# Sums of squares with the ones stationary, and roots that travel by way of HBM, in one layer of a hybrid decoder trunk

## The chip, the core and the metric

The kernel runs on one core of a Trainium2 chip. A core has a matrix engine (TensorE, PE in the profile, which reads its stationary operand by weight loads, PEld), a vector engine (VectorE, DVE), a scalar engine (ScalarE, ACT), a general engine (GpSimd, POOL) and a queue engine (SyncE, SP). Each takes its instructions in order. Transfers between HBM and the on-chip memory are issued from the queues of SP, ACT and POOL. The metric is the device time of one execution in microseconds, lower is better; the median of three runs before is 676.56 us.

## The reference

One decoder layer on 512 tokens of width 1024. After a modulated RMSNorm one projection feeds two token mixers. The second of them, differential attention, is where the change lies:

```python
scores = jnp.einsum('bqhmd,bshmd->bhmqs', qblk, k).astype(jnp.float32) * scale
...
p = jax.nn.softmax(scores, axis=-1)
a = p[:, :, 0] - lam * p[:, :, 1]
return jnp.einsum('bhqs,bshe->bqhe', a.astype(v.dtype), v)
...
out = _rmsnorm(out, subln_g) * (1.0 - lam_init)
```

There are four heads of 128 value columns. Each head's output is normalised for each token: its 128 values are squared and summed, the mean plus a small constant goes under a root, and the values are multiplied by the inverse root, a gain per column and a constant. Both mixers' outputs are then projected, gated and merged, projected again and added to the input; a gated MLP and a last RMSNorm follow.

## The kernel before

Everything is float32; large products are made of three passes over operands split into a high part that TensorE takes at full speed and a low part (`split`, `mm3`: high times high, high times low, low times high). The split of each weight tile is one cast on ScalarE and one subtraction on VectorE.

From line 513 the order of TensorE's instructions is written by hand. `fill(n)` advances a stream of background products (query and key projections, gates of the first mixer `pga`, its branch `pA`, gates of the second `pgd`, its branch `pB`) by n ticks, a tick being three passes of 512 columns; between the ticks the attention's own products are placed. `after(n, fn)` has `fn` issued n ticks later. The orders of VectorE, ScalarE and POOL in this stretch are chosen by a planner from priorities (`tc.high_priority`) and from bounds such as `tc.issue_after`, which keeps an instruction behind another on the same engine.

`diff_values(h)` (line 727) makes a head's output with the value columns on the partitions and the 512 tokens along the free dimension, in the one bank of the tag "v". ScalarE squares it into `sq` and copies it, with the gain, into `of`. STAT_LAG (6 ticks) later `stats` runs:

- Four matmuls (line 746), one for each block of 128 tokens, with the block of squares stationary and one column of ones moving: they leave the sums as a 128x4 block, tokens on partitions, in a "v" bank `pss`.
- `rstd_start` on VectorE (line 156) scales these and adds `e0`, the small constant times the squared softmax denominator, which POOL makes in lines 749 and 750; POOL takes the power of -1/2 (line 158) and four steps that refine it (lines 755 to 758), and writes four columns of the tile `cols`.
- ROW_LAG (8, 8, 6, 7) ticks after the statistic `to_rows` (line 100) turns columns of `cols` on TensorE, ScalarE copies the last 32 rows to `part`, and two DMAs issued from POOL write the four rows to HBM (2 KB) and read them back to all 128 partitions as `rb`, 128x512 (256 KB).
- NORM_LAG (34, 34, 34, 24) ticks after the statistic `spread` multiplies `of` by `rb` on VectorE (line 768) and splits the product into the head's places in `vvh` and `vvl`. For heads 0 to 2 the multiply is kept behind the next head's statistic step (`summed[h + 1]`).

The branch `pB` of the second mixer (`add_merge`, line 958) reads `vvh` and `vvl` of all four heads, head by head. `to_rows` serves the two gates of the residual adds too (`g1`, `g2`).

Of the kernel before, what the change touches and what calls it, by code (L numbers as in the profile page):

```python
# [8 lines left out]
F32 = mybir.dt.float32  # L9
F32R = mybir.dt.float32r  # L10
AF = mybir.ActivationFunctionType
ALU = mybir.AluOpType
PSUM = bass.MemoryType.PSUM

P = 128
# [3 lines left out]
NT = S // P  # L19
DFF = 2816  # L20
FT = DFF // P
EPS = 1e-6
# [5 lines left out]
HP = 100000  # L28
# [6 lines left out]
ROW_LAG = (8, 8, 6, 7)  # L35
# [4 lines left out]
NCOL = 161  # L40
G1COL = NCOL + 16
# [6 lines left out]
def kernel(  # L48
# [19 lines left out]
    nc = tc.nc  # L68
# [3 lines left out]
    def pool(name, bufs=1, space=None, stack=ctx):  # L72
        kw = {} if space is None else {"space": space}
        return stack.enter_context(tc.tile_pool(name=name, bufs=bufs, reuse_waits="tile", **kw))

    cpool = pool("const")
# [3 lines left out]
    dp = pool("rows", space=bass.MemoryType.DRAM)  # L80

    def bank(tag, bufs, shape, name, dt=F32):
        return ps.tile(shape, dt, tag=tag, bufs=bufs, name=name)
# [10 lines left out]
    def vbank(name, shape=(P, S)):  # L94
        return bank("v", 1, list(shape), name)
# [4 lines left out]
    def to_rows(dst, lo, n, name):  # L100
        turned = vbank(name, (P, P))
        nc.tensor.transpose(turned, cols[:, lo + n - P : lo + n], ident)
        part = cpool.tile([32, P], F32, tag="part", name=name + "p")
        with tc.high_priority(offset=2 * HP):
            nc.scalar.copy(part, turned[96:])
        d = dp.tile([n, P], F32, name=name + "d")
        nc.gpsimd.dma_start(d, part[32 - n :])
        nc.gpsimd.dma_start(dst, d.rearrange("k q -> (k q)").partition_broadcast(P))
# [10 lines left out]
    def split(hi, lo, src):  # L119
        return nc.scalar.copy(hi, src), nc.vector.tensor_sub(lo, src, hi.bitcast(F32))  # L120

    def mm3(o, lh, ll, rh, rl, start, stop):
        nc.tensor.matmul(o, lh, rh, start=start, stop=False)  # L123
        nc.tensor.matmul(o, lh, rl, start=False, stop=False)  # L124
        nc.tensor.matmul(o, ll, rh, start=False, stop=stop)  # L125
# [4 lines left out]
    ones = cpool.tile([P, P], F32, name="ones")  # L130
# [5 lines left out]
    mhalf = cpool.tile([P, 4], F32, name="mhalf")  # L136
# [3 lines left out]
    cols = cpool.tile([P, NCOL + 64], F32, name="cols")  # L140
# [8 lines left out]
    root_in = [None]  # L149

    def rstd_start(ssq, n, d, wpool, plus=None):
        ms = wpool.tile([P, n], F32, tag="rs_a", bufs=3, name="ms")
        if plus is None:
            nc.vector.tensor_scalar(ms, ssq, 1.0 / d, EPS, ALU.mult, ALU.add)
        else:
            root_in[0] = nc.vector.scalar_tensor_tensor(ms, ssq, 1.0 / d, plus, ALU.mult, ALU.add)
        r0 = wpool.tile([P, n], F32, tag="rs_c", bufs=3, name="r0")
        nc.gpsimd.tensor_tensor(r0, ms, mhalf[:, :n], ALU.pow)
        return ms, r0
# [74 lines left out]
    def keep_warm(n):  # L234
        for i in range(n):
            nc.tensor.matmul(acc[5][:, :P], ones, ones, start=True, stop=True)
# [12 lines left out]
    nc.gpsimd.affine_select(ddf, ddf, [[-1, 512]], ALU.is_ge, NEG, base=384, channel_multiplier=1)  # L249
    eps = cpool.tile([P, 1], F32, name="eps")  # L250
    nc.gpsimd.memset(eps, EPS)

    keep_warm(10)
    cs = cpool.tile([P, 8], F32, name="cs")
# [56 lines left out]
    for p in range(KT // 2):  # L311
        for hf in range(2) if p == 3 else (None,):
            sl = ALL if hf is None else HALVES[hf]
            sq, xx = (a.rearrange("p (a s) -> p a s", a=2)[:, :, sl] for a in (sqs[p], xT[:, p]))
# [15 lines left out]
    r0 = pp.tile([P, NT], F32, tag="rs_c", bufs=3, name="r0")  # L330
    nc.scalar.activation(r0, stat[:, :, 0], AF.Sqrt, bias=eps, scale=1.0 / D)
    ms = pp.tile([P, NT], F32, tag="rs_a", bufs=3, name="ms")
# [59 lines left out]
    for k in range(KT):  # L392
        n = k + 1
# [24 lines left out]
    ap = pool("att", stack=at)  # L418
# [129 lines left out]
    def after(n, fn):  # L548
        later.append([n, fn])
# [175 lines left out]
    emptied, summed = {}, {}  # L725

    def diff_values(h):
        aTh, aTl = aTs[h]
        o = vbank(f"od{h}")
        for k in range(NT):  # L730
            q0 = k * P
            mm3(
                o[:, q0:], vv[0][:, h, k * P : (k + 1) * P], vv[1][:, h, k * P : (k + 1) * P],
                aTh[:, k * AW + q0 : k * AW + 512], aTl[:, k * AW + q0 : k * AW + 512],
                k == 0, k == NT - 1,
            )
        sq = big.tile([P, S], F32, tag="sq2", name=f"sq{h}")
        of = big.tile([P, S], F32, tag=("kvA", "kvB")[h % 2], name=f"of{h}")
        with tc.high_priority(offset=HP):
            nc.scalar.activation(sq, o, AF.Square)  # L740
            emptied[h] = nc.scalar.activation(of, o, AF.Copy, scale=sublnc)

        def stats():
            pss = vbank(f"pss{h}", (P, NT))
            for n in range(NT):
                nc.tensor.matmul(pss[:, n : n + 1], sq[:, n * P : (n + 1) * P], ones[:, 0:1], start=True, stop=True)
            rs = cols[:, NCOL + NT * h : NCOL + NT * h + NT]
            l0, e0 = sums[h][:, 0], sums[h][:, 1]
            nc.gpsimd.tensor_tensor(e0, l0, l0, ALU.mult)
            nc.gpsimd.tensor_scalar_mul(e0, e0, EPS)  # L750
            with tc.high_priority(offset=HP):
                ms, r0 = rstd_start(pss, NT, P, ap, plus=e0)
                summed[h] = root_in[0]
                t = ap.tile([P, NT], F32, tag="rs_b", bufs=3, name="rt")
                nc.gpsimd.tensor_tensor(t, r0, r0, ALU.mult)
                nc.gpsimd.tensor_tensor(t, t, ms, ALU.mult)
                nc.gpsimd.tensor_scalar_add(t, t, -3.0)
                nc.gpsimd.tensor_tensor(rs, t, r0, ALU.mult)
            last = h == DIFF_HEADS - 1
            rb = big.tile([P, S], F32, tag="sq2", name="rb3") if last else ap.tile([P, S], F32, tag="rb", name=f"rb{h}")  # L760

            def spread():
                with ExitStack() as place:
                    for b in recent:
                        place.enter_context(tc.issue_after(b.ins))
                    if not last:
                        place.enter_context(tc.issue_after(summed[h + 1].ins))
                    nc.vector.tensor_mul(of, of, rb)
                with tc.high_priority(offset=HP), ExitStack() as place:
                    if not last:  # L770
                        place.enter_context(tc.issue_after(emptied[h + 1].ins))
                    split(vv[0][:, h], vv[1][:, h], of)

            after(ROW_LAG[h], lambda: to_rows(rb, NCOL + NT * h, NT, f"rs{h}"))
            after(NORM_LAG[h], spread)

        after(STAT_LAG[h], stats)


# [114 lines left out]
    for s in range(4 * DIFF_HEADS):  # L894
        h, n = divmod(s, NT)
# [368 lines left out]
    ssq, r2, xns = {}, {}, {}  # L1264
# [614 lines left out]
```

## Time and profile before

| | |
|---|---|
| median of three runs | 676.56 us (676.55 to 677.2) |
| profiled execution, first to last instruction | 675.4 us |
| mean granted clock of TensorE | 0.996 |
| sums of squares (line 746), four heads | start at 149.42, 174.56, 199.00, 216.90 us |
| multiply by the roots (line 768) | starts at 178.88, 202.85, 219.85, 235.29 us |
| first `pB` | starts at 238.52 us |

The page gives busy time for each engine, the view of windows the same for stretches of the span with the granted clock of TensorE and the DMA's share. Groups of instructions stand by line, output and inputs. A row of the timeline gives the start, the length, the engine and line, the operation and its shapes, how many were merged (x8), and in brackets how long the engine had been idle and who released it. Starts are the more telling on TensorE, where neighbours overlap. The list of DMA issues gives size and median time from issue to landing. The chain that ended last is merged in the same way. One float32 matmul of these statistics is issued as two passes, each with a weight load, so four stand as x8.

### The profile page before, as it was taken

To read this page: it belongs to the slowest core of one execution; us is meant where nothing else is said; L and a number is where in the kernel's file an instruction comes from. 1 tells how busy PE (TensorE), PEld (TensorE's weight loads), DVE (VectorE), ACT (ScalarE), POOL (GpSimd) and SP (SyncE) were. 2 spreads that over 40 slices of the span, in tenths; PEclk is the share of its full clock that TensorE was granted. 3 is DMA by queue.
4 is the path that set the end of the run, shared out by engine and by line. 5 is a ranking of instruction groups with operands and counts; after the bars stand their busy time and mean duration, and the time that the engine had idled before them with its cause. 6 is when DMAs were issued, how large, how long until landed. Compare 5 with 4: busy or idle time off the path is not lost.

```text
span 675.4 us, 10797 instructions
## 1 busy us (share of the span) xinstructions
PE 665.2 (98%) x4021; PEld 591.5 (88%) x4021; DVE 564.1 (84%) x1005; ACT 400.6 (59%) x704; POOL 85.0 (13%) x111
## 2 busy tenths in 40 slices
PE   8999999999999999999999999999999999999995
PEld 7888888888887888888899999999999998888884
DVE  6988997778767678954899998888888899979996
ACT  7678787465745333233696655556655666665664
POOL 2000000002213100010010211011111004441200
PEclk9999999999999999999999999999999999999998
DMA  9961231445255697568365988797886559996803
GB/s 357 417 235 62 94 95 63 132 149 179 89 170 188 236 314 264 189 185 282 92 123 137 227 201 200 203 214 162 187 198 171 132 187 208 198 203 186 157 0 125
DMA packets 72068, 121.78 MB, mean 180 GB/s; under 512 B 4240, under 2 KB 48432, under 8 KB 72016
## 3 DMA queue, kind: packets, MB, share of 16 engines
q1 hardware_dynamic: 53104, 95.04, 41.4%
q0 software_dynamic: 18624, 25.84, 22.8%
q8 instruction: 31, 0.51, 0.3%
q10 hardware_dynamic: 288, 0.21, 0.1%
q14 instruction: 21, 0.17, 0.1%
HBM read 118.97 MB, written 2.11 MB: 179 GB/s over the span
## 4 chain that ended last, share of the span: by engine, by line
PE 84%; issue 7%; DVE 4%; DMA 1%; ACT 1%; POOL 1%; POOLq 0%; ACTq 0%
PE up L1202 33%; PE dc L1808 7%; PE av L371 3%; PE oc L1262 2%; PE oc L1258 2%; PE pgd L124 2%; PE pgd L123 2%; PE oc L1259 2%; PE pgd L125 2%; PE aqa L368 2%; PE pga L123 1%; PE pga L125 1%; PE pga L124 1%; PE sw L581 1%; PE sd L679 1%
## 5 line engine op out<-in xcount | busy, mean ns | idle before, releaser
L1202 PE MATMUL up<-t,m_whi 128*128 128x256 f32 x512 | 93.1, 283 | 0.0
L1202 PEld LDWEIGHTS up<-t,m_whi 128*128 128x128 f32 x512 | 79.9, 192 | 0.0
L1202 PE MATMUL up<-t,m_wlo 128*128 128x256 f32 x256 | 72.4, 283 | 0.0
L1202 PE MATMUL up<-bh,p_whi 128*128 128x256 f32 x232 | 65.7, 283 | 0.0
L1202 PE MATMUL up<-bl,p_whi 128*128 128x256 f32 x232 | 65.7, 283 | 0.0
L1202 PE MATMUL up<-bh,p_wlo 128*128 128x256 f32 x232 | 65.7, 283 | 0.0
L1202 PEld LDWEIGHTS up<-t,m_wlo 128*128 128x128 f32 x256 | 49.2, 192 | 0.0
L1104 POOL DMA_DIRECT2D s<-in_w_up_dram x21 | 27.0, 1367 | 158.5 <-DMA s<-in_w_up_dram 104.8
L1202 PEld LDWEIGHTS up<-bh,p_whi 128*128 128x128 f32 x232 | 44.5, 192 | 0.0
L1202 PEld LDWEIGHTS up<-bl,p_whi 128*128 128x128 f32 x232 | 44.5, 192 | 0.0
L1202 PEld LDWEIGHTS up<-bh,p_wlo 128*128 128x128 f32 x232 | 44.5, 192 | 0.0
L1132 ACT CAST m_whi<-s 128x1024 fp32r<-128x1024 f32 x31 | 32.5, 1048 | 15.7 <-DVE s L1126 9.1
L795 DVE CUSTOM_DVE_ANT_0 ra<-ra,csb 128x1024 f32<-128x1024 f32 x32 | 38.6, 1219 | 3.8 <-DMA ra<-in_w_ada_t_dram 3.7
L1136 DVE TENSOR_TENSOR m_wlo<-s,m_whi 128x1024 fp32r<-128x1024 f32 x31 | 37.7, 1217 | 1.3 <-ACT m_whi L1132 1.3
L1202 PE MATMUL up<-t,p_whi 128*128 128x256 f32 x176 | 32.2, 283 | 0.0
L1202 PEld LDWEIGHTS up<-t,p_whi 128*128 128x128 f32 x176 | 27.4, 192 | 0.1
L705 ACT ACTIVATE sd<-sd,dmx 128x128 f32<-128x128 f32 (+3 forms) x32 | 17.8, 556 | 14.9 <-DVE dmx L690 14.7
L1132 ACT CAST p_whi<-wa 128x1024 fp32r<-128x1024 f32 x18 | 18.8, 1042 | 12.6 <-PE up L1202 9.0
L1209 ACT ACTIVATE gT<-a,cols 128x512 f32<-128x512 f32 x22 | 17.6, 813 | 13.4 <-DVE a L1244 13.0
L1136 DVE TENSOR_TENSOR p_wlo<-wa,p_whi 128x1024 fp32r<-128x1024 f32 x18 | 22.0, 1222 | 4.0 <-ACT p_whi L1132 2.7
L1202 PE MATMUL up<-t,p_wlo 128*128 128x256 f32 x88 | 24.9, 283 | 0.0
L1126 DVE TENSOR_TENSOR s<-s,wa 128x1024 f32<-128x1024 f32 x20 | 24.3, 1217 | 0.1
(551 smaller groups left out, 2036.4 us busy)
## 6 DMA issues: line engine op xcount, KB each, us to landing
ra<-in_w_ada_t_dram SPq DMA_DIRECT2D x32, 512.0 KB, 4.3
wa<-in_w_up_dram SPq DMA_DIRECT2D x22, 512.0 KB, 4.3
s<-in_w_up_dram SPq DMA_DIRECT2D x21, 512.0 KB, 4.7
s<-in_w_up_dram POOLq DMA_DIRECT2D x21, 512.0 KB, 6.8
adaw<-in_w_ada_t_dram SPq DMA_DIRECT2D x15, 512.0 KB, 9.9
a<-in_w_up_dram SPq DMA_DIRECT2D x11, 512.0 KB, 4.8
b<-in_w_down_dram SPq DMA_DIRECT2D x10, 512.0 KB, 4.0
w<-in_w_first_dram SPq DMA_DIRECT2D x8, 512.0 KB, 9.9
```

The lines of the kernel that those rows point to most:

```text
L123: nc.tensor.matmul(o, lh, rh, start=start, stop=False)
L124: nc.tensor.matmul(o, lh, rl, start=False, stop=False)
L125: nc.tensor.matmul(o, ll, rh, start=False, stop=stop)
L371: nc.tensor.matmul(acc[i], ht[:, t : t + P], wts[k][w][:, S:], start=start, stop=stop)
L705: nc.scalar.activation(pm[m], pm[m], AF.Exp, bias=mx[:, m : m + 1], scale=-1.0, accum_out=(l0, l1)[m])
L795: nc.vector.tensor_tensor_reduce(r, r, csb, 1.0, 0.0, ALU.mult, ALU.add, late_mod[:, idx : idx + 1])
L1104: nc.gpsimd.dma_start(dst, upblock(*blk), accum_op=ALU.add)
L1126: nc.vector.tensor_add(src, src, R[J, "a11" if name == "m6" else "a12"])
L1132: nc.scalar.copy(W[J, name][0], R[J, SRC[name]])
L1136: nc.vector.tensor_sub(lo, R[J, SRC[name]], hi.bitcast(F32))
L1202: nc.tensor.matmul(o[u], w[:, k, cu], b[:, k], start=name in ("p1", "m5", "p2") and k == 0 and x == 0, stop=k == 3 and x == 2, skip_group_ ...
L1808: nc.tensor.matmul((bank2[u] if o is None else o)[:, sl], a[:, q, cu], b[:, q, sl], start=first_mm and x == 0, stop=last_mm and x == 2, sk ...
```

## The change

The sums of squares are taken the other way round: 32 columns of ones are stationary, and each block of 128 tokens moves past them; block n writes partitions 32n to 32n + 31 of `pss`, now 128x128, all 32 with the same row of sums. VectorE copies `pss` whole into `row`; one partition of each 32 is written to HBM as four rows (`back`), and read back as columns, 128x4 (`ssq`), four bytes at a time. The addition of `e0` and the scaling move from VectorE to POOL, followed by the root and its refinement as before, with the constant scaled to suit. The result is written to HBM as columns turned to rows (`d`), four bytes at a time again, and broadcast to `rb`. `to_rows` is no longer used for the heads, its transposes, copies and ROW_LAG fall away there, and the multiply's place (NORM_LAG) is unchanged. All four DMAs are issued from POOL. `summed[h]` is now the copy. A memset fills the columns of `cols` that the roots no longer write, since `to_rows` for `g1` still turns them.

```diff
+    nc.gpsimd.memset(cols[:, NCOL:G1COL], 0.0)
...
         def stats():
-            pss = vbank(f"pss{h}", (P, NT))
+            pss = vbank(f"pss{h}", (P, P))
             for n in range(NT):
-                nc.tensor.matmul(pss[:, n : n + 1], sq[:, n * P : (n + 1) * P], ones[:, 0:1], start=True, stop=True)
-            rs = cols[:, NCOL + NT * h : NCOL + NT * h + NT]
+                nc.tensor.matmul(
+                    pss[32 * n : 32 * n + 32], ones[:, :32], sq[:, n * P : (n + 1) * P], start=True, stop=True,
+                )
+            row = cpool.tile([P, P], F32, tag="part", name=f"ssrow{h}")
+            with tc.high_priority(offset=HP):
+                summed[h] = nc.vector.tensor_copy(row, pss)
+            back = dp.tile([NT, P], F32, name=f"back{h}")
+            nc.gpsimd.dma_start(back, row[0:P:32])
+            ssq = ap.tile([P, NT], F32, tag="rs_a", bufs=3, name=f"ssq{h}")
+            nc.gpsimd.dma_start(ssq, back.rearrange("n q -> q n"))
             l0, e0 = sums[h][:, 0], sums[h][:, 1]
             nc.gpsimd.tensor_tensor(e0, l0, l0, ALU.mult)
-            nc.gpsimd.tensor_scalar_mul(e0, e0, EPS)
-            with tc.high_priority(offset=HP):
-                ms, r0 = rstd_start(pss, NT, P, ap, plus=e0)
-                summed[h] = root_in[0]
-                t = ap.tile([P, NT], F32, tag="rs_b", bufs=3, name="rt")
-                nc.gpsimd.tensor_tensor(t, r0, r0, ALU.mult)
-                nc.gpsimd.tensor_tensor(t, t, ms, ALU.mult)
-                nc.gpsimd.tensor_scalar_add(t, t, -3.0)
-                nc.gpsimd.tensor_tensor(rs, t, r0, ALU.mult)
+            nc.gpsimd.tensor_scalar_mul(e0, e0, EPS * P)
+            nc.gpsimd.tensor_tensor(ssq, ssq, e0, ALU.add)
+            nc.gpsimd.tensor_scalar_mul(ssq, ssq, 1.0 / P)
+            r0 = ap.tile([P, NT], F32, tag="rs_c", bufs=3, name="r0")
+            nc.gpsimd.tensor_tensor(r0, ssq, mhalf, ALU.pow)
+            t = ap.tile([P, NT], F32, tag="rs_b", bufs=3, name="rt")
+            nc.gpsimd.tensor_tensor(t, r0, r0, ALU.mult)
+            nc.gpsimd.tensor_tensor(t, t, ssq, ALU.mult)
+            nc.gpsimd.tensor_scalar_add(t, t, -3.0)
+            nc.gpsimd.tensor_tensor(t, t, r0, ALU.mult)
+            d = dp.tile([NT, P], F32, name=f"rs{h}d")
+            nc.gpsimd.dma_start(d.rearrange("n q -> q n"), t)
...
-            after(ROW_LAG[h], lambda: to_rows(rb, NCOL + NT * h, NT, f"rs{h}"))
+            nc.gpsimd.dma_start(rb, d.rearrange("n q -> (n q)").partition_broadcast(P))
             after(NORM_LAG[h], spread)
```

## The prediction

> **What bounds the kernel now.** I read the page's first part, then the windows around the change, then TensorE's waits after 60 us.
>
> ```profile
> span 675.4 us, 10797 instructions
> PE 665.2 (98%) x4021; PEld 591.5 (88%) x4021; DVE 564.1 (84%) x1005; ACT 400.6 (59%) x704; POOL 85.0 (13%) x111
> ...
> core 0: us, PE busy (x) PEld busy (x) DVE busy (x) ACT busy (x) POOL busy (x), PEclk, DMA share, GB/s
> 118.00:217.00 99.00, 98.73 (x496) 82.69 (x494) 75.50 (x184) 55.84 (x118) 17.85 (x29) 1.00 0.46 147
> 217.00:241.00 24.00, 24.00 (x112) 19.88 (x111) 16.53 (x24) 8.04 (x12) 4.08 (x8) 1.00 0.74 249
> 241.00:294.00 53.00, 53.00 (x236) 43.84 (x235) 44.75 (x62) 17.29 (x25) 2.12 (x3) 1.00 0.72 240
> ...
> 666.00:675.00 9.00, 1.61 (x14) 1.41 (x12) 4.79 (x16) 3.60 (x11) 0.59 (x1) 0.75 0.56 214
> ...
> PE od L124 <- DVE aTl L427: 0.3, 1, 0.3
> ```
>
> TensorE (PE) is busy all the time: in the two windows from 217 to 294 us there is no idle time at all, and after 60 us the only wait named is 0.3 us. Its order is written by hand (line 513), so a microsecond taken from its queue in the differential heads comes off the end, and a microsecond for which it stands still there is added to the end. VectorE (DVE) is second, busy 16.5 of 24 and 44.8 of 53 us; it can catch up a few us, not many. The other engines have room. The profile runs 675.4 us from first to last instruction and the median of the runs is 676.56; I put the 1.2 us of difference around the span in both kernels and apply the sum to the median.
>
> **Part one: TensorE's own work.** Removed are, per head, eight passes of the statistic (an f32 matmul is issued as two passes, so four make x8) and the transpose in to_rows. Added are eight passes with 32 columns of ones stationary.
>
> ```profile
> 149.42 0.95 PE L746 MATMUL pss<-ones,sq 128*128 128x1 f32 x8
> 150.23 0.42 PE L720 MATMUL td<-ident,sd 128*128 128x128 f32 x2
> ...
> 222.38 0.40 PE L125 MATMUL pga<-hThA,wga_l 128*128 128x512 f32 x1
> 222.62 0.27 PE L102 MATMUL rs<-ident,cols 128*128 128x128 f32 x1
> ...
> 222.96 0.39 PE L124 MATMUL pga<-hTlA,wga_h 128*128 128x512 f32 x1
> ...
> 109.27 3.25 PE L632 MATMUL oa<-pT,va 128*64 128x256 f32 x32
> 112.44 1.19 PE L679 MATMUL sd<-qk 128*128 128x128 f32 x8
> ...
> 9.07 2.05 PE av L304 x16
> ...
> 240.56 0.39 PE L123 MATMUL pB<-vvh,wbd 128*128 128x512 f32 x1
> 240.79 0.39 PE L124 MATMUL pB<-vvl,wbd 128*128 128x512 f32 x1
> ```
>
> The old statistic takes 150.23 - 149.42 = 0.81 us from its start to the next start. The transpose: from 222.38 to 222.96 two ordinary matmuls and the transpose take 0.58 us, and two ordinary ones 2 x 0.23 (240.56 to 240.79), so it costs 0.12. The new form has no row. Its nearest row is oa (L632), where the two halves of the columns work in turn: 32 passes in 112.44 - 109.27 = 3.17 us, 99 ns each, though three in four have 256 columns. That is 7168 streamed columns, 0.44 ns a column. At full width, L304 needs 2.05 / 16 = 128 ns for 128 columns, 1.0 ns a column. So column positions do overlap here. [...] Eight passes of 128 columns at 0.44 ns are 0.45 us, and 0.1 for the last, uncovered pass: 0.55. Bounds: no overlap 8 x 0.128 = 1.03, four at a time 0.23. With 0.55 a head saves 0.81 - 0.55 + 0.12 = 0.38 us, four heads **1.5 us**; the bounds are a loss of 4 x 0.10 = 0.4 and a gain of 4 x 0.70 = 2.8.
>
> The Trainium skill (TensorEngine Tiling (Array Packing), Theoretical Speedup and Key Properties) gives up to four times for outputs of at most 32 columns, and says that a change of tiling mode drains the array. By four times the sum here would be the 2.8 us; oa, entered and left once in 3.17 us, shows no drain large enough to see.
>
> The new memset of unused columns of cols runs once on POOL at the start, beside the waits for the first loads and long before its first reader: nothing; uncovered it would cost its own length once, less than one of the POOL steps below (0.20). ScalarE loses four copies and was not the bound: nothing. DVE's small root step (0.16 us) becomes a 128x128 copy (0.29 by the row below): 0.5 us in all, in its idle time; uncovered, 0.5.
>
> **Part two: the way from the sums to the normalised head.** Before it is DVE step, POOL root, PE transpose, ACT copy, DMA out (2 KB), DMA broadcast. Now it is DVE copy, DMA out, DMA in turned to columns, two more POOL steps and the root, DMA out turned to rows, DMA broadcast. All four DMAs are issued from POOL, and each waits for the one before to land. The lag between statistic and use is unchanged.
>
> ```profile
> 174.56 0.95 PE L746 MATMUL pss<-ones,sq 128*128 128x1 f32 x8
> ...
> 202.85 0.68 DVE L768 TENSOR_TENSOR of<-of,rb 128x512 f32<-128x512 f32 x1
> ...
> L690 DVE CUSTOM_DVE_ANT_0 sd<-sd,ddf 128x128 f32<-128x128 f32 x8 | 2.0, 285 | 0.0
> ...
> 201.30 0.15 DVE L156 SCALAR_TENSOR_TENSOR ms<-pss,dls 128x4 f32<-128x4 f32 x1
> ...
> 217.96 0.16 DVE L156 SCALAR_TENSOR_TENSOR ms<-pss,dls 128x4 f32<-128x4 f32 x1
> 219.85 0.69 DVE L768 TENSOR_TENSOR of<-of,rb 128x512 f32<-128x512 f32 x1 [1.73 <-DMA rb<-rs2d]
> ...
> 235.29 0.69 DVE L768 TENSOR_TENSOR of<-of,rb 128x512 f32<-128x512 f32 x1
> 236.48 1.22 DVE L120 TENSOR_TENSOR wgd_l<-wgd,wgd_h 128x1024 fp32r<-128x1024 f32 x1 [0.50 <-ACT wgd_h L120]
> 237.62 0.68 DVE L120 TENSOR_TENSOR vvl<-of,vvh 128x512 fp32r<-128x512 f32 x1
> ...
> 201.55 1.95 POOL L158 TENSOR_TENSOR r<-ms,mhalf 128x4 f32<-128x4 f32 x1 [13.44 <-DVE ms L156]
> ...
> 204.46 0.20 POOL L758 TENSOR_TENSOR cols<-rt,r 128x4 f32<-128x4 f32 x1
> ...
> 208.56 0.61 POOL L107 DMA_DIRECT2D rs2d<-rs2p  x1
> 213.14 0.56 POOL L108 DMA_DIRECT2D rb<-rs2d  x1 [3.97 <-DMA rs2d<-rs2p]
> 218.20 1.05 POOL L158 TENSOR_TENSOR r<-ms,mhalf 128x4 f32<-128x4 f32 x1 [4.50 <-DVE ms L156]
> ...
> 220.72 0.20 POOL L758 TENSOR_TENSOR cols<-rt,r 128x4 f32<-128x4 f32 x1
> 223.52 0.60 POOL L107 DMA_DIRECT2D rs3d<-rs3p  x1 [2.60 <-ACT rs3p L105]
> 227.34 0.58 POOL L108 DMA_DIRECT2D rb<-rs3d  x1 [3.22 <-DMA rs3d<-rs3p]
> ...
> s<-in_w_up_dram POOLq DMA_DIRECT2D x21, 512.0 KB, 6.8
> ...
> rb<-rs0d POOLq DMA_DIRECT2D x1, 256.0 KB, 3.5
> rb<-rs1d POOLq DMA_DIRECT2D x1, 256.0 KB, 4.9
> rb<-rs2d POOLq DMA_DIRECT2D x1, 256.0 KB, 6.7
> rb<-rs3d POOLq DMA_DIRECT2D x1, 256.0 KB, 5.4
> ```
>
> Prices. A 2 KB write up to the next issue on POOL: 213.14 - 208.56 = 4.6 and 227.34 - 223.52 = 3.8, mean **4.2**. The root on POOL: 204.66 - 201.55 = 3.1 and 220.92 - 218.20 = 2.7, mean 2.9, and two more steps at 0.3: **3.5**. The broadcast: mean of the four rows, **5.1**. The two turned DMAs also move 2 KB, but in 512 pieces of 4 bytes; no row shows that. Below, the 2 KB row without any surcharge (3.8); above, the 512 KB add from POOL, 6.8 and 0.5 to the next issue. By size the 2 KB row is the nearer, so I take 4.2 and put 0.7 on it for the pieces: **4.9** each, an estimate. From the first write to the broadcast's issue: 4.2 + 4.9 + 3.5 + 4.9 = **17.5 us**.
>
> Heads 0 and 1 have the most time; head 1 has 202.85 - 174.56 = 28.3 us from statistic to multiply, where copy, way and broadcast end some 26 us after it (its copy, like its old step, may run late): they hold. Head 2: its copy runs where the step at 201.30 did, so the first write is issued at 201.65 and the broadcast at 219.15. Head 3: copy at 217.8, first write ready at 218.2. POOL's queue is in order; head 2's broadcast was called for earlier, so I put it ahead, and head 3 waits behind it until 219.7. Then the broadcast of head 3 is issued at 237.2 and lands at 242.3; before, it landed at 227.34 + 5.4 = 232.7 and the multiply ran at 235.29. Now multiply, weight split and low part (0.69 + 1.22 + 0.69) follow on DVE from 242.3 to **244.9**. TensorE reads that low part in the first pB at 240.79, or 240.4 with head 3's saving: it stands for 4.5 us, where it had 2.5 us to spare (237.62 + 0.68 = 238.3).
>
> Queued behind the waiting multiply of head 3 on DVE are the weight split for the next gate (done at 244.2, ahead of its reader, which stands behind pB) and products for the late modulation, that nobody needs soon. Behind that of head 2 (219.85, now until 219.15 + 5.1 = 224.3) stands the step that empties a pA bank for the next pA; what TensorE waits there lies ahead of the stall at pB and shortens it by as much, since the broadcast of head 3 doesn't wait for TensorE. SP's queue is not passed. POOL's next customer, the transfer of the g1 rows, is behind head 3's broadcast or beside it; its reader is the scaling of the output weights, a stage later. The e0 products run while a DMA is under way.
>
> **Sum:** saving 1.5, stall 4.5: 3.0 us slower, 676.56 + 3.0 = **679.6 us**.
>
> **Rivals.**
> (a) *The lag covers it.* With the low prices (3.8 per DMA step, POOL 3.3, broadcast 3.5) the 14.7 us from 218.2 end at 232.9, head 2 is out of the way, the broadcast lands at 236.4 and the low part is there at 238.4 to 239: no stall. Then only part one counts: 676.56 - 1.5 = 675.1, and 673.8 with four positions at a time. For it speaks that the old broadcast came 2.6 us before its multiply; against it, that head 2's multiply already waited 1.73 us for its broadcast with a chain two DMAs shorter. It decides below about 14.5 us from first write to broadcast at a mean broadcast, 16 at the shortest.
> (b) *The 4-byte pieces are dear.* At 7.3 (6.8 and 0.5) a turned DMA and the other steps as above, the way takes 22.3 us: head 2's broadcast is issued at 224.0, head 3's at 246.8, landing at 251.9, low part 254.5, a stall of 14.1: 676.56 + 12.6 = 689.2. For it speaks the DMA share of 0.74 in that window, against it the small volume.
> (c) *The stall costs clock too.* In the last window TensorE idles most of 9 us and the granted clock is 0.75; if it were 0.75 for 9 us after the stall, 2.3 us would come on top: 681.9. The Trainium skill (TensorE: Matmul & The Clock Gate, Part 1) has the clock halve after an idle window of some 3.4 us and stay so for another, which would be 1.7 us, 681.3; the trace has a lowered clock after an idle stretch, but only at the end.
> (d) *The positions don't overlap.* Part one then loses 0.4; with a covered chain 677.0, no change.
>
> **How the numbers follow.** A measurement of this kernel can tell about 0.2%, 1.35 us, from no change. Forecast with stalls of 3 to 8 us: 0.45; (c) 0.07; (b) 0.10: slower, and with them 0.62. (a) 0.24, most of it just past 0.2%: 0.21 faster, 0.03 the same. (d), and a stall of 0.2 to 2.8 us that about eats the saving: 0.14 the same. So faster 0.21, same 0.17, slower 0.62. The range goes from the covered chain, 674.8, to a stall of 10 us, 685.0; it leaves out the best packing and the dearest pieces.
>
> **What would show it.** Right: a gap in PE before the fourth head's matmul of the first pB, released by DVE's vvl, and DVE's multiply (L768 before) waiting on the broadcasts of heads 2 and 3. The statistic's block should be 0.5 to 0.6 us from start to next start. Wrong: no idle PE in 217 to 294 us (then a), POOL steps between the DMAs under 4 us apart (a) or over 6 (b), or a planner that moves DVE's other work so that a stall arises elsewhere.

## The result, and the profile after

| | before | after |
|---|---|---|
| median of the runs | 676.56 us (676.42 to 677.2) | 701.66 us (699.24 to 703.22) |
| ratio, 95% interval | | 1.0365 (1.0353 to 1.0377) |
| profiled execution, first to last instruction | 675.4 us | 699.9 us |

The changed kernel is 25.1 us slower, where 3.0 were forecast. The page's first part and TensorE's waits after 60 us, of the changed kernel (waits: engine, instruction, what it waited for, us in total, times, longest):

```profile
span 699.9 us, 10802 instructions
...
PE 671.9 (96%) x4017; PEld 593.7 (85%) x4017; DVE 564.6 (81%) x1005; ACT 398.5 (57%) x700; POOL 95.1 (14%) x128
```

```profile
PE pA L123 <- DVE ta L835: 6.6, 1, 6.6
PE pss L747 <- ACT of L742: 6.5, 1, 6.5
PE pB L123 <- ACT vvh L120: 5.2, 1, 5.2
PE pB L124 <- DVE vvl L120: 0.3, 1, 0.3
```

TensorE, which had waited 0.3 us after 60 us, now waits 18.6, in three places. Only the last, at `pB`, was forecast as a stall. The place where all extra time has been spent is found by an instruction behind the heads whose surroundings did not change, the first pass of the output projection (`oc`). Its row in the answer for that tile, before:

```profile
L1258 PE MATMUL oc<-wo_h,mg0h x16: 389/389/476, 292.9 to 303.0; 128*128 128x512 f32 x16
```

and after:

```profile
L1270 PE MATMUL oc<-wo_h,mg0h x16: 388/389/477, 317.7 to 327.8; 128*128 128x512 f32 x16
```

It starts 317.7 - 292.9 = 24.8 us later, and the span is 24.5 us longer: all of it arises ahead of 318 us. The chain that ended last, cut to the stretch from 185 to 262 us of the changed kernel (start, us, what), says by which steps:

```profile
189.40 12.82 DMA wga<-in_w_tiles_dram
...
209.76 3.00 DMA back<-ssrow
...
213.05 2.62 DMA ssq<-back
...
221.88 9.96 DMA rs2d<-rt
...
232.69 4.05 DMA back<-ssrow
237.02 2.57 DMA ssq<-back
...
243.11 9.64 DMA rs3d<-rt
...
253.33 7.29 DMA rb<-rs3d
```

No matmul stands in it. Two things are long that had no such length in the forecast: the turned write of the roots (`rs2d`, `rs3d`: 9.96 and 9.64 us for 2 KB), and a load of a weight tile, `wga`, 12.82 us. The list of DMA issues in the same stretch (KB each, median us to landing) puts the turned read beside the turned write:

```profile
ssq<-back POOLq DMA_DIRECT2D x2, 2.0 KB, 2.6
rs1d<-rt POOLq DMA_DIRECT2D x1, 2.0 KB, 10.5
rs2d<-rt POOLq DMA_DIRECT2D x1, 2.0 KB, 10.0
```

Both move 512 pieces of 4 bytes. Read, they cost 2.6 us; written, 10.0 and 10.5 (`rs3d`: 9.6). And the weight load? The view of windows, with the DMA's busy share and GB/s at the end of a row, for two stretches in which a turned write was under way:

```profile
189.00:199.00 10.00, 8.99 (x45) 7.40 (x43) 2.11 (x5) 0.87 (x2) 1.89 (x2) 1.00 0.42 68
...
244.00:253.00 9.00, 9.00 (x41) 7.34 (x40) 4.79 (x7) 0.94 (x2) 0.00 (x0) 1.00 0.89 30
```

From 244 to 253 us the DMA engines were busy for 0.89 of the time and moved 30 GB/s; the window from 241 to 294 before shows 0.72 and 240 GB/s. From 189 to 199 they moved 68 GB/s and were busy for only 0.42, with `wga`, issued at 189.40 right behind `rs1d` (188.14), still under way. So the busy share is not high in both windows, and what `wga` waits for inside the transfer no view shows. The load is felt at ScalarE's cast of that tile: `of` and `sq` of head 2 stand behind it on ScalarE, and the sums behind them on TensorE.

```profile
202.30 1.04 ACT L120 CAST wga_h<-wga 128x1024 fp32r<-128x1024 f32 x1 [11.78 <-DMA wga<-in_w_tiles_dram]
```

So the hypothesis after this reading has two parts: the turned write is **long**, and it **holds up other transfers**. The experiments take them apart.

### The profile page after: what moved, and what is told of

The parts are those of the page before. It is cut to its first block, busy times and chain, and to the rows that moved or that the text cites. A ratio compares the mean times of both kernels' runs of the same rounds, so it can differ in the third digit from the quotient of the medians.

```text
span 699.9 us, 10802 instructions
## 1 busy us (share of the span) xinstructions
PE 671.9 (96%) x4017; PEld 593.7 (85%) x4017; DVE 564.6 (81%) x1005; ACT 398.5 (57%) x700; POOL 95.1 (14%) x128
## 4 chain that ended last, share of the span: by engine, by line
PE 76%; DMA 9%; issue 8%; DVE 4%; POOL 2%; ACT 1%; POOLq 0%; ACTq 0%; DVEq 0%
PE up L1214 32%; PE dc L1820 6%; PE av L372 3%; PE oc L1274 2%; PE oc L1270 2%; PE oc L1271 2%; DMA wga<-in_w_tiles_dram 2%; PE pgd L124 2%; PE pgd L123 2%; PE pgd L125 2%; PE aqa L369 2%; DMA rs2d<-rt 1%; DMA back<-ssrow 1%; DMA rs3d<-rt 1%; DMA ssq<-back 1%
## 5 line engine op out<-in xcount | busy, mean ns | idle before, releaser
L1221 ACT ACTIVATE gT<-a,cols 128x512 f32<-128x512 f32 x22 | 17.6, 813 | 13.4 <-DVE a L1256 13.0
```

The lines of the kernel that those rows point to most:

```text
L1221: nc.scalar.activation(grow(j), av[J][:, u], AF.Identity, bias=cv[:, 66 + j : 67 + j], scale=cv[:, 44 + j : 45 + j])
```

## The experiments

**Is it the turned write? The return path alone put back.** The sums as in the change, with `back` and the turned read, but the roots go into `cols` and back to rows by TensorE's transpose and the plain 2 KB write, as before:

```diff
-ROW_LAG = (8, 8, 6, 7)
+ROW_LAG = (18, 18, 18, 18)
...
-            d = dp.tile([NT, P], F32, name=f"rs{h}d")
-            nc.gpsimd.dma_start(d.rearrange("n q -> q n"), t)
...
-            nc.gpsimd.dma_start(rb, d.rearrange("n q -> (n q)").partition_broadcast(P))
+            after(ROW_LAG[h], lambda: to_rows(rb, NCOL + NT * h, NT, f"rs{h}"))
```

> The changed kernel, but the roots go back to rows by the old transpose, copy and 2 KB write (18 ticks after the statistic), so that only the write of 512 four-byte pieces is gone; the new sums and the turned read stay. Theory A (the turned write is what costs: it lands after 9.2 to 10.5 us and holds up other loads meanwhile): 674.5 to 678.5 us, no wait of TensorE over 2 us. Rival B (the longer way with one more wait on POOL for each head is enough, whatever the write): still above 690 us, with stalls at pA and pB.

Measured: 684.24 us, ratio 1.0103 (1.0088 to 1.0119). TensorE's two longest waits in this run (a third, at the low part, is 0.3 us):

```profile
PE pB L123 <- ACT vvh L120: 3.4, 1, 3.4
PE rs L102 <- POOL cols L768: 1.2, 1, 1.2
...
```

The waits at `pss` and `pA` are gone, and no `wga` load takes more than 3.7 us. The turned write, against the old return, accounts for 701.66 - 684.24 = 17.4 of the 25 us; what is left, 684.24 - 677.0 = 7.2 against the kernel before in the same session, goes with the sums' way out and in (and with the later place of the transpose). Neither of the two times expected came: the write is the larger part, but not all of it. This run also has the one stall of the forecast, at `pB`, 3.7 us against 4.5.

**Does it hurt when nobody waits for it?** The kernel before, unchanged in what it computes and waits for, with the same 512 pieces written once per head to a buffer that nothing reads:

```diff
+            extra = dp.tile([NT, P], F32, name=f"ex{h}")
+            nc.gpsimd.dma_start(extra.rearrange("n q -> q n"), rs)
```

> The kernel before with one addition: for each head the roots are also written to HBM as 512 four-byte pieces, and nobody reads them or waits for them. Theory A (the write holds up the other loads): loads from SP beside it land 6 to 9 us late, TensorE waits for weights at least once, 680 to 695 us. Rival B (only the latency in the chain counts, the transfer itself disturbs nobody): 676.5 to 677.5 us, loads as before.

Measured: 689.86 us, ratio 1.0189 (1.0173 to 1.0204): 8 KB that no one reads cost 12.9 us. The answer for the tile `ex` in this run gives the landing times, the two longest waits of TensorE say who paid, and a window in which a write was under way shows the DMA:

```profile
DMA to landing us min/median/max: 9.8/10.5/12.2
```

```profile
PE pss L746 <- ACT of L741: 4.7, 1, 4.7
PE pga L123 <- ACT ta L808: 2.5, 1, 2.5
...
```

```profile
211.00:222.00 11.00, 11.00 (x57) 8.94 (x56) 7.72 (x13) 5.54 (x11) 2.67 (x4) 1.00 0.76 33
```

The wait at `pss` is the one of the changed kernel. ScalarE's `of` stands behind the cast of `wga` on its queue, and that load took up to 12.4 us (before: 5.5 at most). The loads are issued from SP, the write from POOL; the DMA engines were busy 0.76 of those 11 us for 33 GB/s. Transfers of POOL's own queue are held as well: the four rows of the roots (`rs0d` to `rs3d`), issued behind the unread write, land in 8.6 to 12.0 us instead of 3.3 to 4.5. So holding up is a cost by itself.

**What about the pieces is dear: their number, their size, or that they lie side by side?** Three variants of the unread write: the same 512 pieces of 4 bytes set 512 bytes apart, the same set 64 bytes apart, and 128 pieces of 16 bytes (a token's four roots together) side by side:

```diff
+            extra = dp.tile([NT, P, P], F32, name=f"ex{h}")
+            nc.gpsimd.dma_start(extra[:, :, 0].rearrange("n q -> q n"), rs)
```

```diff
+            extra = dp.tile([NT, P, 16], F32, name=f"ex{h}")
+            nc.gpsimd.dma_start(extra[:, :, 0].rearrange("n q -> q n"), rs)
```

```diff
+            extra = dp.tile([P, NT], F32, name=f"ex{h}")
+            nc.gpsimd.dma_start(extra, rs)
```

> As the unread write, but each four-byte piece lies 512 bytes from the next, so that no two pieces share a line of HBM. If the dearness comes from neighbours that write into the same line: landing under 5 us and 677 us. If it comes from the pieces themselves (their number or their size): landing 9 to 10.5 us and the time of the other unread write within 1 us.

> The kernel before with the unread write of 512 four-byte pieces per head, the pieces 64 bytes apart (side by side they landed in 10.5 us and gave 689.9; 512 bytes apart in 2.5 us and 677.3). If what is shared by neighbouring pieces is 64 bytes or less, the write lands in 2.4 to 2.9 us, the weight loads in their usual 3 to 4, and the time is 677 to 677.6. If it is larger, up to 512 bytes, up to eight pieces still meet in it: landing above 4 us, weight loads held up, time from 679 up to 690.

> As the unread write, same 2 KB, but laid down as 128 pieces of 16 bytes, each partition's own four roots side by side. If the price goes by the number of pieces: landing about 4 to 5 us and at most 2 us over the kernel before. If it goes by the 2 KB or by any write under 512 bytes alike: landing over 8 us and the time of the four-byte write.

| unread write per head | lands in (min/median/max) | median | ratio (95%) |
|---|---|---|---|
| 512 x 4 bytes, side by side | 9.8/10.5/12.2 | 689.86 | 1.0189 (1.0173 to 1.0204) |
| 512 x 4 bytes, 512 bytes apart | 2.3/2.5/2.9 | 677.33 | 1.0009 (1.0000 to 1.0019) |
| 512 x 4 bytes, 64 bytes apart | 2.3/2.6/2.9 | 677.27 | 1.0009 (1.0000 to 1.0018) |
| 128 x 16 bytes, side by side | 1.8/2.8/3.9 | 677.34 | 1.0009 (0.9999 to 1.0018) |

The same number of the same small pieces costs at most 0.2% once they lie 64 bytes apart. So neither their number alone nor their size alone makes the write dear; 512 four-byte pieces from different partitions, side by side, do.

**The change with a cheap write.** The roots are written as they lie, 16 bytes a token, so that the chain keeps its four DMAs and loses only the dear form:

```diff
-            d = dp.tile([NT, P], F32, name=f"rs{h}d")
-            nc.gpsimd.dma_start(d.rearrange("n q -> q n"), t)
+            d = dp.tile([P, NT], F32, name=f"rs{h}d")
+            nc.gpsimd.dma_start(d, t)
...
-            nc.gpsimd.dma_start(rb, d.rearrange("n q -> (n q)").partition_broadcast(P))
+            nc.gpsimd.dma_start(rb, d.rearrange("q n -> (q n)").partition_broadcast(P))
```

> The changed kernel whole, with the write of the roots laid down as 128 pieces of 16 bytes instead of 512 of four that share lines; chain, waits and bytes stay. The order of the roots in HBM is then another, so the heads are scaled by the wrong tokens' roots. Theory A (that write is the cost): landing about 2.8 us instead of 9.7, time 674.5 to 680 us, with a stall of 0 to 4 us left at pB from the longer way. Rival B (four waiting DMAs on POOL cost most of it anyway): over 690 us.

Measured: 685.49 us, ratio 1.0131 (1.0117 to 1.0145). The DMA steps on POOL in this run (start, us; in brackets how long POOL had been idle, and for what):

```profile
202.43 0.59 POOL L754 DMA_DIRECT2D back<-ssrow  x1 [9.57 <-DVE ssrow L752]
...
220.07 0.55 POOL L786 DMA_DIRECT2D rb<-rs2d  x1 [3.19 <-DMA rs2d<-rt]
220.61 0.59 POOL L754 DMA_DIRECT2D back<-ssrow  x1
...
240.49 0.55 POOL L786 DMA_DIRECT2D rb<-rs3d  x1 [5.66 <-DMA rs3d<-rt]
```

Head 2's way is 220.07 - 202.43 = 17.6 us, head 3's 240.49 - 220.61 = 19.9; head 3's first write goes out right behind head 2's broadcast. This is the kernel that the forecast had in mind, with the heads scaled by other tokens' roots, and head 2's way is nearly the forecast's 17.5. That this one sum agrees is luck: its root took 5.6 us (210.60 to 216.24) where 3.5 were forecast, and its three other steps 12.0 where 14.0 were. The time, 8.9 us over the kernel before, lies between the two that were expected: a way of four waiting DMAs is too long even with a cheap write.

**Holding up and length, each alone, in the change.** Two further edits of the kernel with the cheap write. In the first the dear write is added, behind the cheap one, and nobody reads it (meant as holding up alone). In the second the cheap write is made three cheap transfers in a row (length alone):

```diff
             nc.gpsimd.dma_start(d, t)
+            extra = dp.tile([NT, P], F32, name=f"ex{h}")
+            nc.gpsimd.dma_start(extra.rearrange("n q -> q n"), t)
```

```diff
+            d1 = dp.tile([P, NT], F32, name=f"ca{h}")
+            nc.gpsimd.dma_start(d1, t)
+            d2 = dp.tile([P, NT], F32, name=f"cb{h}")
+            nc.gpsimd.dma_start(d2, d1)
-            nc.gpsimd.dma_start(d, t)
+            nc.gpsimd.dma_start(d, d2)
```

> As the kernel with the cheap write, and the dear write of 512 four-byte pieces is issued right behind it, unread: nobody waits for it, so it only holds up others. The roots are in the wrong order here too. If the holding up is the larger part: 688 to 700 us. If the latency of the write in the chain is the larger part: 676 to 683 us.

> As the kernel with the cheap write, but three cheap transfers in a row, each waiting for the one before, take the place of one: some 9 us of latency and no holding up. The roots are in the wrong order here too. If the latency is the larger part: 688 to 700 us, with stalls at pA and pB as in the changed kernel but none behind a weight load. If the holding up is the larger part: 677 to 684 us.

Measured: 701.08 us, ratio 1.0366 (1.0350 to 1.0382), with the dear write beside; 694.83 us, ratio 1.0268 (1.0254 to 1.0282), with three cheap ones. TensorE's longest waits with the dear write beside:

```profile
PE pA L123 <- DVE ta L837: 6.6, 1, 6.6
PE pss L747 <- ACT of L742: 5.7, 1, 5.7
```

and with three cheap ones:

```profile
PE pA L123 <- DVE ta L839: 4.9, 1, 4.9
PE pB L123 <- ACT vvh L120: 4.3, 1, 4.3
...
```

The dear write, merely beside the way, brings back the whole loss, and by three routes: `wga` is held again (5.7 us at `pss`); the cheap write that left just before it lands 8.8 to 10.5 us after its issue for heads 0 to 2, instead of 2.7 to 3.5; and head 3's broadcast, issued right behind it, lands after 12.5 us instead of 3.3. So this run does not hold the length of the way fixed. Three cheap transfers take 10.35 us for head 2 (216.46 to 226.81), as long as the dear write, and there is no wait behind a weight load: no `wga` needs over 5.8 us. That is the length alone, at 694.83. The two do not add up: the dear write beside the way costs 701.08 - 685.49 = 15.6, the length 9.3, and both together, in the changed kernel, 16.2. So neither is the larger part by itself: 694.83 lies in the range expected if the length were, and 701.08 just above the one expected if the holding up were. The split depends on the order. In one order, from differences of medians:

| step | us |
|---|---|
| before to four waiting DMAs, cheap write | 685.49 - 676.57 = 8.9 |
| the write's length (10 us instead of 3 to 6) | 694.83 - 685.49 = 9.3 |
| the rest, from three cheap transfers to the dear write | 701.66 - 694.83 = 6.8 |

The three cheap transfers were 1.6 us longer than the dear write for head 3 (236.89 to 248.70 against 243.11 to 253.33), so the split between the last two steps is good to about that, in this order. That the rest is the holding up is read from the wait at `pss`, which only the kernels with the dear write have.

**Is the new form of the sums worth anything without the trip by HBM?** The kernel before with the new sums, VectorE's copy, and one transpose on TensorE that turns the four rows back to columns, two ticks after the sums; the rest as before:

```diff
-            pss = vbank(f"pss{h}", (P, NT))
+            pss = vbank(f"pss{h}", (P, P))
...
-                nc.tensor.matmul(pss[:, n : n + 1], sq[:, n * P : (n + 1) * P], ones[:, 0:1], start=True, stop=True)
+                nc.tensor.matmul(
+                    pss[32 * n : 32 * n + 32], ones[:, :32], sq[:, n * P : (n + 1) * P], start=True, stop=True,
+                )
+            row = cpool.tile([P, P], F32, tag="part", name=f"ssrow{h}")
+            with tc.high_priority(offset=HP):
+                nc.vector.tensor_copy(row, pss)
...
+            after(2, lambda: roots(row, rb))
...
+            nc.tensor.transpose(psc, row, ident)
...
-                ms, r0 = rstd_start(pss, NT, P, ap, plus=e0)
+                ms, r0 = rstd_start(psc[:, 0:P:32], NT, P, ap, plus=e0)
```

> A version of my own: the sums with the ones stationary as in the change, their copy turned to columns by one transpose on TensorE two ticks later, and from there the kernel before (root step on DVE, POOL, transpose, one 2 KB write, broadcast). If TensorE's saving is real and only the way by HBM spoiled it: 4 x (0.81 - 0.36 - 0.12) = 1.3 us less, about 675.2 to 675.7 us. If the four column positions save nothing on the whole: 676.6 or more.

Measured: 676.70 us, ratio 1.0000 (0.9991 to 1.0009). TensorE waits once after 60 us, for head 1's copy, as the timeline of the two engines shows:

```profile
176.93 0.29 DVE L751 COPY ssrow<-pss 128x128 f32<-128x128 f32 x1
...
177.28 0.33 PE L759 MATMUL psc<-ident,ssrow 128*128 128x128 f32 x1 [0.75 <-DVE ssrow L751]
```

VectorE reaches head 1's copy late, behind other work, and TensorE stands 0.75 us for it. The saving that was expected here, 1.3 us, was put too high: from the `td` behind head 0's sums to that behind head 1's it is 174.70 - 149.76 = 24.94 us, where the kernel before needs 175.36 - 150.23 = 25.13. That is 0.19 us a head, 0.8 in four, about what the one wait takes back. Three runs looked for the place where it doesn't: all turns four ticks behind the sums (with the transpose to rows two ticks nearer), then head 1's alone, then head 1's four and head 2's three ticks.

```diff
-            after(2, lambda: roots(row, rb))
+            after(4, lambda: roots(row, rb))
...
-ROW_LAG = (8, 8, 6, 7)
+ROW_LAG = (6, 6, 4, 5)
```

```diff
-            after(2, lambda: roots(row, rb))
+            after((2, 4, 2, 2)[h], lambda: roots(row, rb))
```

```diff
-            after((2, 4, 2, 2)[h], lambda: roots(row, rb))
+            after((2, 4, 3, 2)[h], lambda: roots(row, rb))
```

> The new sums with one turn by TensorE as in the run at 676.70, but the turn is placed four ticks behind the sums instead of two, and the transpose to rows two ticks earlier behind it. If the 0.75 us that TensorE stood there before the turn of head 1 was only DVE's copy being late, it is gone, and four heads save 4 x (0.45 - 0.12) = 1.3 us: 675.2 to 675.6. If the wait turns up elsewhere (the roots come two ticks later, the multiply of heads 2 and 3 has 1 to 2 us to spare), the time stays at 676.3 to 677.

> The new sums with one turn by TensorE, as in the run at 676.70, but head 1's turn four ticks behind its sums instead of two; nothing else is moved. Head 1 is where TensorE stood 0.75 us for DVE's copy of the sums. If that was the only thing that ate the saving, TensorE stands nowhere after 60 us, and 4 x (0.45 - 0.12) = 1.3 us are saved against before: 675.2 to 675.6. If DVE's work is placed anew and TensorE waits elsewhere, 676 to 677, no difference from before.

> The run before, at 677.47, with head 2's turn three ticks behind its sums instead of two: there TensorE stood 0.77 us for DVE's copy, where it had stood for head 1's before. If DVE's lateness is what eats the saving, TensorE stands nowhere now and the time is 675.2 to 675.8. If DVE has no room for four copies of 0.29 us at the places where TensorE wants them, the wait turns up at the next reader of DVE's work and the time is 676.4 to 677.6.

Measured: 680.10 us, ratio 1.0059 (1.0046 to 1.0072); 677.47 us, ratio 1.0026 (1.0011 to 1.0041), its runs spread from 676.38 to 680.71; 677.60 us, ratio 1.0017 (1.0008 to 1.0026). The waits after 60 us of the three, in that order:

```profile
PE rs L102 <- POOL cols L771: 2.3, 2, 1.6
```

```profile
PE psc L759 <- DVE ssrow L751: 0.8, 1, 0.8
```

```profile
PE rs L102 <- POOL cols L771: 1.8, 1, 1.8
PE psc L759 <- DVE ssrow L751: 1.1, 1, 1.1
```

The wait does not go, it moves: to the next reader of the roots, or from head 1's turn to head 2's. The first of the three, at 680.10, lies above both times expected. In these four placements what TensorE saves it stands for, at VectorE's copy or at the roots; that VectorE has no place at all for four more copies is likely and not shown. No version here beats the kernel before.

## Why the prediction was right or wrong

The direction and the frame were right, the size was not: 3.0 us forecast, 25.1 measured. Its steps in order:

**TensorE sets the end, and its stalls add.** Right. All idle time that is new stands in the four waits after 60 us, and behind `oc` nothing is lost or won.

**Part one.** Right in sign and near in size, for other reasons than the forecast gave. TensorE's rows around the sums of head 1 in the changed kernel, and the pass ahead of them in the kernel before:

```profile
173.60 0.39 PE L125 MATMUL pga<-hThA,wga_l 128*128 128x512 f32 x1
173.92 0.42 PE L747 MATMUL pss<-sq,ones 128*32 128x128 f32 x8
174.28 0.44 PE L721 MATMUL td<-ident,sd 128*128 128x128 f32 x2
```

```profile
174.33 0.39 PE L125 MATMUL pga<-hThA,wga_l 128*128 128x512 f32 x1
```

From start to next start the block takes 0.36 us, not 0.55; no run shows the 0.1 that the forecast put on it for a last, uncovered pass. But TensorE enters it late: it starts 0.32 us after the pass ahead of it, where the old block started 0.23 after (174.33 to 174.56). So a part of the saving is lost at the entry, where the forecast had seen no drain. From the `td` behind head 0's sums to that behind head 1's it is 25.13 us before, 174.28 - 149.57 = 24.71 in the changed kernel, and 174.60 - 149.78 = 24.82 in the one with the return path put back. So a head saves 0.42 us, of it 0.31 by the new sums: 1.7 us in four heads, against 1.5.

How many positions work at a time stays open. The forecast took 1.0 ns a column as the price without overlap, but the passes behind that figure each load 128 stationary columns, and the old sums, which load as many and stream one column, still take 0.81 / 8 = 0.10 us a pass. The new passes load 32 columns. So the block may be faster by its lighter loads, by overlap, or by both, and no run takes these apart. The Trainium skill (TensorEngine Tiling (Array Packing), Theoretical Speedup) gives up to four times; against the forecast's 1.03 us the block alone is 2.9 times as fast, with the late entry 1.03 / 0.45 = 2.3 times.

**Part two, the way.** This is where it fell. The steps, by the rows of POOL's timeline in the changed kernel:

```profile
221.88 0.86 POOL L770 DMA_DIRECT2D rs2d<-rt  x1 [0.29 <-POOL rt L768]
232.14 0.56 POOL L786 DMA_DIRECT2D rb<-rs2d  x1 [9.39 <-DMA rs2d<-rt]
232.69 0.60 POOL L754 DMA_DIRECT2D back<-ssrow  x1
...
243.11 0.85 POOL L770 DMA_DIRECT2D rs3d<-rt  x1 [0.29 <-POOL rt L768]
253.33 0.57 POOL L786 DMA_DIRECT2D rb<-rs3d  x1 [9.38 <-DMA rs3d<-rt]
```

| step, us | forecast | head 2 | head 3 |
|---|---|---|---|
| plain write to next issue | 4.2 | 213.05 - 209.76 = 3.3 | 237.02 - 232.69 = 4.3 |
| turned read | 4.9 | 215.74 - 213.05 = 2.7 | 239.67 - 237.02 = 2.7 |
| root on POOL | 3.5 | 221.88 - 215.74 = 6.1 | 243.11 - 239.67 = 3.4 |
| turned write to broadcast's issue | 4.9 | 232.14 - 221.88 = 10.3 | 253.33 - 243.11 = 10.2 |
| sum | 17.5 | 22.4 | 20.6 |

**The failed step is the term "4.9 each" for the two turned DMAs, with its upper bound of 7.3.** The forecast called the 2 KB row the nearest by size and put 0.7 on it; read, the pieces need less than even the lower bound of 3.8 (2.7), written they lie above the upper one (10.3 and 10.2). One price was set for a read and a write that differ by a factor of four, and the bound was taken from a large transfer, which says nothing about many small pieces. The rival (b) had the right mechanism with a chance of 0.10, but the same two errors: it priced both at 7.3. The root on POOL was mis-sized too where its steps ran slowly: 6.1 us for head 2, against 3.5.

**And a term was missing: what the write does to others.** "SP's queue is not passed" was true and not enough. A load that SP had issued, at 189.40, landed late. ScalarE's cast behind `wga` held up `of`, `sq` and the sums of head 2. By how much shows when the forecast's schedule is set beside the two kernels:

| us | forecast | changed kernel | cheap write |
|---|---|---|---|
| head 2's first write issued | 201.65 | 209.76 | 202.43 |
| head 2's broadcast issued | 219.15 | 232.14 | 220.07 |
| head 3's first write issued | 219.7 | 232.69 | 220.61 |
| head 3's broadcast issued | 237.2 | 253.33 | 240.49 |
| head 3's multiply starts | 242.3 | 260.64 | 243.80 |
| its low part is there | 244.9 | 263.08 | 246.24 |

The low part comes 18.2 us later than forecast: 8.1 because head 2 starts late (the held load), 4.9 in head 2's way, 3.1 in head 3's, 2.2 in the broadcast (7.3 instead of 5.1), and 0.1 less elsewhere. With a cheap write the first three rows hold to within 1 us; head 3's way is then 2.4 longer than forecast, for its root took 6.9 us (227.25 to 234.20) and its cheap write 6.3 to the next issue.

**The order on POOL, and VectorE behind its waiting multiply.** Right. `back` of head 3 stands at 232.69, directly behind head 2's broadcast at 232.14. VectorE's multiplies wait for the broadcasts of heads 2 and 3, as its timeline shows:

```profile
236.59 0.69 DVE L780 TENSOR_TENSOR of<-of,rb 128x512 f32<-128x512 f32 x1 [11.70 <-DMA rb<-rs2d]
237.20 0.68 DVE L835 SCALAR_TENSOR_TENSOR ta<-ta,pA 128x512 f32<-128x512 f32 x1
...
260.64 0.69 DVE L780 TENSOR_TENSOR of<-of,rb 128x512 f32<-128x512 f32 x1 [11.86 <-DMA rb<-rs3d]
```

Behind the first stands the step that empties the bank for `pA`: TensorE's 6.6 us. The forecast said that such a wait shortens the stall at `pB` by as much, since the way of head 3 doesn't wait for TensorE. The chain of waits bears that out, in that no matmul stands between 209 and 262 us; no run tried it alone.

**Rival (c), the clock, belonged in the sum.** TensorE's rows around its longest wait:

```profile
237.94 0.80 PE L123 MATMUL pA<-outah,wba_h 128*128 128x512 f32 x1 [6.63 <-DVE ta L835]
238.53 0.63 PE L124 MATMUL pA<-outal,wba_h 128*128 128x512 f32 x1
...
243.65 0.58 PE L124 MATMUL pgd<-hTlA,wgd_h 128*128 128x512 f32 x1
244.07 0.39 PE L125 MATMUL pgd<-hThA,wgd_l 128*128 128x512 f32 x1
```

From 238.53 to 244.07 us the passes are 0.43 us apart, then 0.23 again: 13 passes, 13 x 0.20 = 2.6 us for one stall, close to the 2.3 that the rival gave. The granted clock from 237.9 to 244.1 us is 0.50. The stalls at `pss` and `pB` have such tails too. Counted with their first passes and set against the same passes at full clock, the three cost an estimated 2.4, 2.9 and 2.9 us. With them TensorE's account nearly closes: 18.6 of waits and 8.2 at half clock, less 1.7 saved, are 25.1 us, where `oc` starts 24.8 later. The tail of the last stall has nothing left to hide behind:

```profile
262.04 0.79 PE L123 MATMUL pB<-vvh,wbd 128*128 128x512 f32 x1 [5.17 <-ACT vvh L120]
263.14 0.80 PE L124 MATMUL pB<-vvl,wbd 128*128 128x512 f32 x1 [0.30 <-DVE vvl L120]
```

TensorE reads the fourth head's low part in the changed kernel at 263.14 (240.79 before), 22.35 us late; `oc` starts 24.8 us late. So 2.45 us come between the two, where the wait list has nothing. With the cheap write the same pair gives 246.29 - 240.79 = 5.5 and 300.5 - 292.9 = 7.6: 2.1 us. There the whole sum is 5.5 + 2.1 = 7.6, against 3.0 of the forecast, which had 2.4 less for head 3's way and left out the clock. The Trainium skill (TensorE: Matmul & The Clock Gate, Part 1) has half clock from an idle window of about 3.4 us until a busy one. Here it lasted 6.1 us from the first pass at 237.94, and beside the unread write a stall of 2.5 us, shorter than that window, was followed by it as well.

**Rivals (a) and (d)** are refuted in their prices: even with a cheap write the way is too long for the lag, and part one saves 1.7 us where (d) had it lose 0.4. Whether the positions overlap is not shown. The 1.2 us around the span were nearly right (701.66 - 699.9 = 1.8).

**What would show it.** The gap ahead of the fourth head's first `pB` is there, though TensorE waits first for the high part (5.2 us) and then 0.3 for the low one that was named. POOL's steps over 6 us pointed to rival (b), as the forecast had said they would.

## What to carry to other kernels

When a small tile has to be turned on its way through HBM, turn it in the read, or keep what a partition writes together in one piece, and look at the spacing of the pieces before their number. What was read so here was 2 KB into 128x4; turning the roots in the broadcast's read was not tried. A small transfer is to be priced twice, by its own time and by what it does to other transfers under way; an unread copy in the unchanged kernel shows the second price. A stall of several microseconds on TensorE has a tail at half clock, which belongs in the sum.

## What the runs showed of the hardware

- **Small writes side by side.** 512 four-byte pieces written side by side land in 9.2 to 12.2 us; in two windows meanwhile the DMA engines were 0.76 and 0.89 busy for 33 and 30 GB/s, in a third 0.42 for 68. The same pieces 64 or 512 bytes apart land in 2.3 to 2.9 us, 128 pieces of 16 bytes side by side in 1.8 to 3.9 unread and 2.7 to 5.7 in the way, and four-byte reads in 2.6 to 4.4. The Trainium skill (DMA: Bandwidth & Descriptors, Specifications) says that below 512 bytes a DMA engine reads, modifies and writes back. That would fit pieces that wait for their neighbours' turn at the same stretch of HBM, which no run shows; size alone it cannot be, since pieces set apart are as small. Open are the spacings between 4 and 64 bytes, and whether it is the neighbourhood or the number of pieces per 2 KB that counts: the 16-byte pieces were only 128.
- **What it does to other queues.** A 512 KB load from SP that takes 3.3 us in the median landed in up to 12.8 us in the changed kernel and in 12.4 beside the unread write.
- **Half clock.** Stalls of 2.5 us (beside the unread write) to 6.6 us were followed by passes 0.43 us apart; after those of 1.0 and 1.5 us with the cheap write there were none. POOL's root steps took 0.2 us in some places and 1.0 to 1.3 in others (6.1 against 3.4 us for a whole root); what makes the difference was not tried.
